# Combinations in four steps, gating two iterations behind its products, and work moved between engines in a two-layer hybrid trunk

## The chip, the cores and the metric

The kernel runs on 1 core of one Trainium2 chip. The metric is the device time of one execution in microseconds (us); smaller is better. Engines are named as in the profile: PE is TensorE, DVE is VectorE, ACT is ScalarE, POOL is GpSimd, and SP is the engine that issues most DMAs.

## What is computed

Two trunk layers over 1024 latent and 128 context tokens of width 1024, in fp32. What matters here, from the reference:

```python
def modulate(x, shift, scale):
    return layer_norm(x) * (1 + scale) + shift
# each of the two layers:
#   h = LN(x) * (1 + scale1) + shift1
#   cols = h @ w_in -> four mixers of 256 channels: mLSTM, pooling, gated MLP, SSD
#   x = LN_1(alpha * x + gate1 * (concat(mixer outputs) @ w_out))
#   h = LN(x) * (1 + scale2) + shift2
#   up-projection to 2 * 2816 -> centred depthwise conv (3) -> SiLU gate -> down-projection
#   x = LN_2(alpha * x + gate2 * ConvFFN(h))
```

## The kernel before, in words

**Tiling.** There are nine token tiles of 128 (tiles 0 to 7 latent, tile 8 context). Activations that feed products lie transposed in two SBUF buffers, `HH` (the part of a value that the fast fp32 product keeps) and `HL` (the rest); weights are split the same way by `wprep` (L141 to L143: DMA into `wr`, cast to `wh` on ACT, difference `wl` on POOL or DVE), and each product is three matmuls: high by high, high by low, low by high. Moving operands are 512 columns wide in most stages and HB = 290 in the FFN's up-projection; HT = 580 is two of those.

**Order.** A scheduler sets the order of each engine's instructions from the order of the code and a model of the times; `pin` keeps the instructions it is put around in the order of the code. Each engine then runs its own list in that order, so that an instruction that waits holds up all behind it. DMAs stand in the lists too: nearly all on SP, nine of the first layer on ACT.

**A layer, stage by stage**, with the lines that are touched:

- *Gating* (the loop over i in 0 to NT that calls `gate_mm`, `gate_a`, `ssd_y`, `ssd_e`, `gate_b`). `gate_mm` is 24 matmuls of 512 columns. `gate_a` takes their tanh and makes the gates. `ssd_y` sums the SSD's output of tile i in `yp`. `gate_b` of the tile before multiplies by the gate (L904), sums squares (L907), scales (L912), transposes on PE (L917) and writes the tile's columns of `HH` and `HL` (L919 to L924). The pooled and gated parts are loaded from DRAM (`pg`) and only split.
- *Out-projection and LN1* (loop after `project`): `project` makes a tile's product with `wo`, `residual` adds the input (L986, L987) and takes statistics, `affine` normalises and applies gain (DVE, L992) and bias (POOL, L993), stores x, a second norm follows on ACT (L250), and `to_ht` transposes (L262), modulates (L272), fills `HH` and `HL` (L274, L277) and spills the tile to DRAM as `hs` (L276, a DMA on SP). `stats` ends on POOL: a power (L221) and the negated product of mean and rstd (L233).
- *Up-projection.* Two of the 22 feature tiles f (`NP = 2`) are computed plainly. The other 20 are computed by `seven`, with seven half products in place of eight; those need sums and differences of activation parts. `combos` makes these from `hs`: per (b, kp) two row tiles `hr` are loaded with four DMAs (L1036, L1037) of 290 KB, four DVE operations combine them (L1046 to L1049), and `hi_lo` splits three results into TH and TL (L1027, L1028; one low part on DVE, two on POOL). Four further calls ("first") load x1 and x3 again and write their difference over the second half of HH and HL (L1042). `pieces` prepares the weight sums of an f on POOL (`sw`, L1092) and DVE. `conv` is the depthwise convolution.
- *Down-projection*: 7 groups of feature tiles by 9 token tiles. Between tiles a generator `ada` computes modulation vectors by steps (loads `wa` of 256 KB, then matmuls L199 and L207). It has 60 steps in layer 0 (20 for this layer, 40 for the next) and 20 in layer 1. Three steps are taken per two tiles from the third group on; what is left is drained at once before the second-last group.
- *LN2* in the last group: residual (zr, L1336; the add L1337 on DVE for the first half of the columns and on POOL for the second), statistics, gain and bias, then in layer 0 the next layer's norm and `to_ht`, in layer 1 the output. `stats` uses DVE's bn_stats (L227); `stats_s` has ACT sum the values and the squares (L240, L242). Layer 0 uses `stats` throughout, layer 1 `stats_s` for tiles 0 to 6.

## Time and profile before

| | |
|---|---|
| median of 3 runs | 2888.89 us (2887.58 to 2893.52) |
| profiled execution, its own time | 2894.44 us |
| its span in the trace | 2892.7 us |
| mean granted TensorE clock | 0.971 of full speed |
| PE busy | 2735.3 us, 95% |
| DVE busy | 1872.7 us, 65% |
| POOL busy | 1184.3 us, 41% |
| ACT busy | 1082.3 us, 37% |

The profile is of one execution. The clock of TensorE has two levels here, 2.4 GHz (shown as 1.00) and 1.2 GHz (0.50). PE counts as busy while a matmul is in flight, at either level, so that a PE that is 95% busy can still lose more than 5%: the number of matmuls in a stretch tells more than the busy time. A wait in the trace is put down to the instruction that released it.

### The profile page before, as it was taken

To read this page: it belongs to the slowest core of one execution; us is meant where nothing else is said; L and a number is where in the kernel's file an instruction comes from. 1 tells how busy PE (TensorE), PEld (TensorE's weight loads), DVE (VectorE), ACT (ScalarE), POOL (GpSimd) and SP (SyncE) were. 2 spreads that over 40 slices of the span, in tenths; PEclk is the share of its full clock that TensorE was granted. 3 is DMA by queue.
4 is the path that set the end of the run, shared out by engine and by line. 5 is a ranking of instruction groups with operands and counts; after the bars stand their busy time and mean duration, and the time that the engine had idled before them with its cause. 6 is when DMAs were issued, how large, how long until landed. Compare 5 with 4: busy or idle time off the path is not lost. (4 is left out here: it accounts for less than half of the span.)

```text
span 2892.7 us, 42560 instructions
## 1 busy us (share of the span) xinstructions
PE 2735.3 (95%) x16432; PEld 2415.6 (84%) x16432; DVE 1872.7 (65%) x3093; ACT 1082.3 (37%) x1960; POOL 1184.3 (41%) x903
## 2 busy tenths in 40 slices
PE   7999998998999999999979999989989999999996
PEld 2888886788999999877668889767889999998785
DVE  4736759565877777443495476685478777764347
ACT  3522343264444444411054234333553444443113
POOL 2534635364333332221484365354543333323137
PEclk9999999999999999999999999999999999999998
DMA  6334332444222223443523343324542222235323
GB/s 247 112 117 137 111 97 77 152 147 130 90 77 69 69 69 113 182 136 120 165 89 90 118 127 104 108 81 153 148 128 77 81 72 69 69 138 181 121 67 117
DMA packets 164891, 329.28 MB, mean 114 GB/s; under 512 B 23408, under 2 KB 81296, under 8 KB 164688
## 3 DMA queue, kind: packets, MB, share of 16 engines
q1 hardware_dynamic: 163392, 321.84, 34.1%
q10 hardware_dynamic: 1296, 4.72, 0.4%
q8 instruction: 129, 2.11, 0.3%
q14 instruction: 74, 0.61, 0.1%
HBM read 257.00 MB, written 69.50 MB: 113 GB/s over the span
## 5 line engine op out<-in xcount | busy, mean ns | idle before, releaser
L147 PE MATMUL ps<-wl,HH 128*128 128x512 f32 (+1 forms) x1152 | 394.3, 391 | 2.3 <-POOL wl L143 2.3
L147 PE MATMUL ps<-wh,HL 128*128 128x512 f32 (+1 forms) x1152 | 388.8, 392 | 5.5 <-POOL HL L277 5.5
L147 PE MATMUL ps<-wh,HH 128*128 128x512 f32 x1080 | 373.5, 401 | 13.1 <-ACT wh L142 8.8
L143 POOL TENSOR_TENSOR wl<-wr,wh 128x1024 fp32r<-128x1024 f32 (+2 forms) x80 | 204.8, 2564 | 347.6 <-ACT wh L142 320.5
L155 PE MATMUL pf<-HH,wh 128*128 128x386 f32 (+2 forms) x928 | 313.6, 338 | 2.7 <-DVE bt L654 2.7
L147 PE MATMUL pf<-HL,wh 128*128 128x386 f32 (+2 forms) x928 | 308.4, 332 | 0.0
L147 PE MATMUL pf<-HH,wl 128*128 128x386 f32 (+2 forms) x928 | 307.7, 332 | 0.0
L1115 PE MATMUL ps<-th,wh 128*128 128x290 f32 x960 | 287.0, 299 | 8.0 <-ACT th L1027 5.5
L1115 PE MATMUL ps<-tl,wh 128*128 128x290 f32 x960 | 287.8, 300 | 1.6 <-DVE tl L1028 1.6
L1115 PE MATMUL ps<-th,wl 128*128 128x290 f32 x960 | 287.3, 299 | 0.0
L147 PEld LDWEIGHTS ps<-wh,HH 128*128 128x128 f32 x1080 | 203.5, 190 | 76.1 <-DVE acc L1262 11.8
L147 PEld LDWEIGHTS ps<-wh,HL 128*128 128x128 f32 x1152 | 218.7, 190 | 54.9 <-POOL HL L277 7.0
L147 PEld LDWEIGHTS ps<-wl,HH 128*128 128x128 f32 x1152 | 219.4, 191 | 50.7 <-POOL wl L143 2.7
L1262 DVE TENSOR_TENSOR acc<-acc,ps 128x512 f32<-128x512 f32 x180 | 115.6, 682 | 198.3 <-PE ps L147 198.3
L1092 POOL TENSOR_TENSOR sw<-wr 128x512 f32<-128x512 f32 x40 | 56.4, 1409 | 440.2 <-DMA wr<-in_wup 258.3
L1115 PE MATMUL ps<-HH,wh 128*128 128x290 f32 x640 | 192.0, 300 | 4.2 <-DVE s L1143 4.2
L1115 PE MATMUL pf<-HH,wh 128*128 128x290 f32 x640 | 190.8, 299 | 3.6 <-ACT HH L1027 3.6
L1115 PE MATMUL pf<-HL,wh 128*128 128x290 f32 x640 | 191.4, 299 | 2.5 <-POOL HL L1028 2.5
L1115 PE MATMUL ps<-HL,wh 128*128 128x290 f32 x640 | 191.6, 299 | 0.0
L1115 PE MATMUL ps<-HH,wl 128*128 128x290 f32 x640 | 191.3, 299 | 0.0
L1115 PEld LDWEIGHTS ps<-th,wh 128*128 128x128 f32 x960 | 183.0, 191 | 9.5 <-ACT th L1027 6.0
L1115 PE MATMUL pf<-HH,wl 128*128 128x290 f32 x640 | 190.0, 297 | 0.0
(338 smaller groups left out, 6856.8 us busy)
## 6 DMA issues: line engine op xcount, KB each, us to landing
wr<-in_wup SPq DMA_DIRECT2D x88, 512.0 KB
wa<-in_w_ada SPq DMA_DIRECT2D x160, 256.0 KB
act<-cv SPq DMA_DIRECT2D x44, 577.0 KB
ar<-act SPq DMA_DIRECT2D x44, 577.0 KB
wr<-in_wdn SPq DMA_DIRECT2D x44, 512.0 KB
e<-rb SPq DMA_DIRECT2D x72, 256.0 KB
wr<-in_wfm SPq DMA_DIRECT2D x28, 512.0 KB
hr<-hs SPq DMA_DIRECT2D x48, 290.0 KB
```

The source lines that it names most:

```text
L143: eng.tensor_tensor(lo[:, :n], raw, hi.bitcast(F32)[:, :n], SUB)
L147: T.matmul(out, l, r, start=start, stop=stop)
L155: b = T.matmul(out, whk, xh, start=k == 0, stop=False)
L1092: G.tensor_tensor(s1, rv[:, h0], rv[:, h1], ADD)
L1115: T.matmul(out, x[:, ks], y[:, k], start=first and k + n == 0, stop=k == 3 and n == 2, skip_group_check=not first)
L1262: V.tensor_tensor(o, o, p[h], ADD)
```

## The change

Eight edits, all in one step:

1. `stats` and `stats_s` end on DVE instead of POOL (the negated mean times rstd, and the mean).
2. The spill of `to_ht` is issued from ACT's list instead of SP's; in the last iterations of LN1 the transposes are pinned.
3. `gate_b` runs two iterations behind `gate_a`; its loads move with it, into buffers of their own (`load_pg`).
4. `project` takes a list of tiles, and tiles 0 and 1 go side by side over k.
5. The bias of LN1 is added on DVE for tiles 7 and 8.
6. The plain product of f = 0 moves into LN1's last two iterations.
7. `combos` keeps every part in a small buffer of its own: 16 loads per layer instead of 24, all issued in one go; the difference x1 that the combinations need is also what goes over the second half of HH and HL, so that nothing is loaded again. Two of three low parts are made on DVE. The sum tile `sw` is one buffer, and the last combination borrows it.
8. `ada` takes two steps after each tile from the second group on; LN2 adds both halves and all biases on DVE and uses `stats_s` for tiles 0 to 6 in both layers.

```diff
@@ stats, stats_s
-        G.tensor_scalar(nm, mv[:, 0:1], rs, -1.0, MUL, MUL)
+        V.tensor_scalar(nm, mv[:, 0:1], rs, -1.0, MUL, MUL)
...
-        G.tensor_scalar(sums[:, 0:1], sums[:, 0:1], -1.0 / D, None, MUL)
+        V.tensor_scalar(sums[:, 0:1], sums[:, 0:1], -1.0 / D, None, MUL)
...
-        G.tensor_tensor(nm, sums[:, 0:1], rs, MUL)
-        return rs, nm
+        V.tensor_tensor(nm, sums[:, 0:1], rs, MUL)
+        return rs, nm, sums[:, 0:1]
@@ to_ht
-                T.transpose(p[:, j * P:(j + 1) * P], xh[:, (4 * h + j) * P:(4 * h + j + 1) * P], ident)
+                hold(T.transpose(p[:, j * P:(j + 1) * P], xh[:, (4 * h + j) * P:(4 * h + j + 1) * P], ident))
...
-                Q.dma_start(out=spill[:, ks, c0:c0 + P], in_=hf)
+                S.dma_start(out=spill[:, ks, c0:c0 + P], in_=hf)
@@ gating
-            pg = [mp.tile([P, 2, P], F32, tag="kt", name="pg", bufs=3) for _ in range(2)]
...
-            Q.dma_start(out=pg[0], in_=pl_d[l][:, :, tok(i)])
-            Q.dma_start(out=pg[1], in_=gu_d[l][:, :, tok(i)])
...
+        def load_pg(i):
+            pg = [mp.tile([P, 2, P], F32, tag=t, name="pg", bufs=n) for t, n in (("kt", 3), ("hs", 2))]
+            Q.dma_start(out=pg[0], in_=pl_d[l][:, :, tok(i)])
+            Q.dma_start(out=pg[1], in_=gu_d[l][:, :, tok(i)])
+            return pg
...
-            if i > 0:
-                gate_b(i - 1, *ga.pop(i - 1))
+            if 1 <= i <= NT:
+                pgs[i - 1] = load_pg(i - 1)
+            if i > 1:
+                gate_b(i - 2, ga.pop(i - 2), pgs.pop(i - 2))
@@ out-projection, LN1
+        def project(tiles):
+            ps_ = [[ps(), ps()] for _ in tiles]
             for k in range(KD):
...
+                for i, p in zip(tiles, ps_):
...
-            G.tensor_tensor(x, x, lnb, ADD)
+            (V if i >= 7 else G).tensor_tensor(x, x, lnb, ADD)
...
+            if i == 0:
+                pq[0], pq[1] = project((0, 1))
+            elif 1 < i < NT:
+                pq[i], = project((i,))
...
+            if i == NT:
+                plain(0, 0)
...
+            if i > NT:
+                plain(0, 1)
+                plain(0, 2)
...
+                to_ht(l, 1, i - 2, z, op, pf if i < NT else ps, spill=hs_d[l],
+                      **({"hold": pin} if i >= NT else {}))
@@ combinations
+        def combos(b, r):
             t1, t2 = slice(HB * b, HB * (b + 1)), slice(HT + HB * b, HT + HB * (b + 1))
...
+            for kp in range(2):
+                n = 2 * b + kp
+                ka, kb = slice(2 * kp, 2 * kp + 2), slice(4 + 2 * kp, 6 + 2 * kp)
...
+                for dst, ks, t in ((x1, ka, t1), (x3, ka, t2), (x2, kb, t2), (x4, kb, t1)):
+                    Q.dma_start(out=dst, in_=hs_d[l][:, ks, t])
+                pin(V.tensor_tensor(x1, x3, x1, SUB))
+                V.tensor_tensor(x3, x2, x3, SUB)
+                V.tensor_tensor(x2, x2, x1, SUB)
+                V.tensor_tensor(x4, x2, x4, SUB)
+                for j, x, eng in ((0, x2, V), (1, x3, G), (2, x4, V)):
+                    hi, lo = tbuf(6 * n + 2 * j), tbuf(6 * n + 2 * j + 1)
+                    hi_lo(hi, lo, x, eng)
...
-            s1, s4 = (up_.tile([P, 512], F32, tag="sw", name="sw", bufs=2) for _ in range(2))
+            s1, s4 = halves(sum_tile())
...
+        plain(1, 0)
         nxt = []
         prep = pieces(NP, nxt)
         next(prep)
+        plain(1, 1)
+        plain(1, 2)
+        t1s = [row_tile("hr").rearrange("p (k c) -> p k c", k=4) for b in range(2)]
+        for b in range(2):
+            combos(b, t1s[b])
+        plain(0, 3)
+        plain(1, 3)
         next(prep)
         for b in range(2):
-            for kp in range(2):
-                combos(b, kp, False)
+            t2 = slice(HT + HB * b, HT + HB * (b + 1))
+            hi_lo(HH[:, 0:4, t2], HL[:, 0:4, t2], t1s[b])
...
-        for b in range(2):
-            for kp in range(2):
-                combos(b, kp, True)
@@ down-projection, LN2
-                    if gi > 1:
+                    if gi > 0:
                         next(ada, None)
-                        if i % 2:
-                            next(ada, None)
+                        next(ada, None)
...
-                        (G if h else V).tensor_tensor(o[:, hs], o[:, hs], z, ADD)
-                    rq[i - 1] = stats(o, tp) if more or i >= CTX else stats_s(o, tp)
+                        V.tensor_tensor(o[:, hs], o[:, hs], z, ADD)
+                    rq[i - 1] = stats_s(o, tp) if i < CTX else stats(o, tp)
...
-                        (G if i % 2 else V).tensor_tensor(o, o, lnb, ADD)
+                        V.tensor_tensor(o, o, lnb, ADD)
```

Lines of the changed kernel have larger numbers than those of the kernel before (L276 stays, L912 becomes L915, L993 becomes L1000, L1115 becomes L1146). Three places of the order follow.

SP's list in layer 0, from the end of LN1 on, before (`hs` written by L276 is the spill, `hr` the loads for the combinations, `wr` weights, `xmid` the stored x):

```order
L276 DMA hs_85<-hf 128x4x128
L141 DMA wr<-in_wup 128x1024
L1077 DMA wr<-in_wup 128x1024
L1078 DMA wr<-in_wup 128x1024
L276 DMA hs_85<-hf 128x4x128 x2
L994 DMA xmid_71<-x 128x1024 x2
L276 DMA hs_85<-hf 128x4x128 x4
L1036 DMA hr<-hs_85 128x2x290
L1037 DMA hr<-hs_85 128x2x290
```

The same place of SP's list now (`tc`, `hr` and `sw` are all loads of parts for the combinations):

```order
L141 DMA wr<-in_wup 128x1024 x2
L1074 DMA sw<-hs_85 128x2x290
L1108 DMA wr<-in_wup 128x1024
L1001 DMA xmid_71<-x 128x1024
L1109 DMA wr<-in_wup 128x1024
L1001 DMA xmid_71<-x 128x1024
L1074 DMA tc<-hs_85 128x2x290
L1074 DMA hr<-hs_85 128x2x290
L1074 DMA tc<-hs_85 128x2x290 x2
```

The spills have left the list, and the loads stand right behind the two last stores of x.

PE's list in layer 0 where `ada` was drained before the second-last group of the down-projection, before:

```order
L147 MATMUL ps<-wh,HL 128x512 x2
L207 MATMUL ps<-pairs,wa 128x2 x4
L199 MATMUL ps<-wa,condw 32x512 x8
L207 MATMUL ps<-pairs,wa 128x2 x4
L199 MATMUL ps<-wa,condw 32x512 x8
L207 MATMUL ps<-pairs,wa 128x2 x4
L147 MATMUL ps<-wh,HH 128x512 x2
```

PE's list now, around the last steps of `ada` in layer 0:

```order
L199 MATMUL ps<-wa,condw 32x512 x2
L147 MATMUL ps<-wh,HH 128x512
L147 MATMUL ps<-wl,HH 128x512
L147 MATMUL ps<-wh,HL 128x512
L147 MATMUL ps<-wh,HH 128x512 x2
L147 MATMUL ps<-wl,HH 128x512
```

No two groups of L199 stand together any more; the products of a token tile lie between them.

PE's list in layer 0 where the first f of `seven` meets its first combination, before:

```order
L1115 MATMUL ps<-HL,wh 128x290
L1115 MATMUL ps<-HH,wl 128x290
L1115 MATMUL ps<-th_5975,wh 128x290
L1115 MATMUL ps<-tl_5978,wh 128x290
L1115 MATMUL ps<-th_5975,wl 128x290
```

The same meeting now:

```order
L1146 MATMUL pf<-HL,wh 128x290
L1146 MATMUL pf<-HH,wl 128x290
L1146 MATMUL ps<-tc,wh 128x290 x6
L1146 MATMUL ps<-tc,wl 128x290
L1146 MATMUL ps<-tc,wh 128x290
```

Before, the half product just ahead of the combination's was the first one on plain activations; now three of the plain ones (the last of them on the difference in HH and HL, in `pf`) come ahead of it.

## Rows read from the trace of the kernel before

**Rows 1.** Stretches: us, busy of PE, PEld, DVE, ACT, POOL (instructions), clock, DMA, GB/s.

```profile
430.00:522.00 92.00, 78.45 (x398) 64.77 (x397) 82.66 (x157) 34.52 (x88) 47.91 (x45) 0.93 0.27 83
626.00:640.00 14.00, 8.86 (x46) 8.26 (x45) 10.99 (x12) 8.73 (x15) 12.19 (x10) 0.76 0.62 174
690.00:740.00 50.00, 40.19 (x236) 38.37 (x235) 41.29 (x48) 25.58 (x38) 19.67 (x12) 0.83 0.44 135
800.00:850.00 50.00, 50.00 (x375) 50.00 (x375) 39.56 (x47) 20.70 (x32) 18.38 (x10) 1.00 0.20 67
1374.00:1395.00 21.00, 16.00 (x51) 5.32 (x52) 2.32 (x6) 2.10 (x3) 4.97 (x4) 0.67 0.71 234
1460.00:1512.00 52.00, 37.70 (x207) 32.05 (x206) 49.30 (x87) 32.56 (x68) 47.30 (x45) 0.87 0.27 102
...
2052.00:2066.00 14.00, 9.03 (x45) 8.21 (x44) 10.50 (x11) 8.32 (x14) 12.16 (x11) 0.76 0.61 182
2120.00:2160.00 40.00, 29.80 (x180) 27.86 (x179) 32.72 (x33) 20.07 (x30) 18.03 (x11) 0.87 0.41 130
2839.00:2868.00 29.00, 28.77 (x124) 22.88 (x122) 25.66 (x34) 18.00 (x27) 24.63 (x25) 1.00 0.18 70
2868.00:2893.00 25.00, 0.00 (x0) 0.00 (x0) 20.24 (x24) 6.45 (x9) 19.14 (x14) 0.54 0.31 126
```

**Rows 2.** What PE waited for over the span: us in total, times, longest us.

```profile
PE ps L917 <- DVE yp L912: 19.8, 18, 3.0
...
PE pf L262 <- ACT z L250: 10.1, 2, 5.1
...
PE pf L262 <- ACT acc L250: 5.8, 4, 2.1
```

**Rows 3.** One line, DVE's L907 in gating: shortest, median and longest ns.

```profile
L907 DVE SCALAR_TENSOR_TENSOR th<-yp x36: 275/292/2364, 440.8 to 1941.1; 128x128 f32<-128x128 f32 x36
```

**Rows 4.** PE's timeline at LN1's end, layer 0: start us, us, idle before.

```profile
632.49 1.97 PE L262 MATMUL pf<-ident,z 128*128 128x128 f32 x8 [5.14 <-ACT z L250]
```

**Rows 5.** ACT's timeline there.

```profile
629.12 1.06 ACT L142 ACTIVATE wh<-wr 128x1024 fp32r<-128x1024 f32 x1 [0.96 <-DMA wr<-in_wup]
...
631.21 1.23 ACT L250 ACTIVATE z<-x,nm,rs 128x1024 f32<-128x1024 f32 x1
```

**Rows 6.** SP's timeline behind LN1, layer 0: the first load for the combinations.

```profile
661.36 0.46 SPq L1036 DMA_DIRECT2D hr<-hs  x1
```

**Rows 7.** What DVE waited for from 640 to 740: us, times, longest.

```profile
DVE hr L1046 <- DMA hr<-hs: 22.2, 3, 18.5
```

**Rows 8.** What PE waited for from 690 to 740, its longest wait.

```profile
PE ps L1115 <- ACT th L1027: 2.8, 1, 2.8
```

**Rows 9.** PE's timeline at `ada`: between tiles (1325.89), then drained.

```profile
1325.89 1.07 PE L199 MATMUL ps<-wa,condw 128*32 128x512 f32 x8
...
1373.15 0.95 PE L207 MATMUL ps<-pairs,wa 128*128 128x2 f32 x8
1374.03 1.38 PE L199 MATMUL ps<-wa,condw 128*32 128x512 f32 x8
1378.99 4.56 PE L199 MATMUL ps<-wa,condw 128*32 128x512 f32 x8 [3.58 <-DMA wa<-in_w_ada]
...
1386.03 6.94 PE L199 MATMUL ps<-wa,condw 128*32 128x512 f32 x16
...
1394.62 0.70 PE L147 MATMUL ps<-wh,HH 128*128 128x512 f32 x2
```

**Rows 10.** One line, LN2's add on either engine: shortest, median, longest ns.

```profile
L1337 DVE TENSOR_TENSOR acc<-acc,zr x18: 632/681/2041, 1442.6 to 2874.4; 128x512 f32<-128x512 f32 x18
L1337 POOL TENSOR_TENSOR acc<-acc,zr x18: 1264/1676/2337, 1442.8 to 2875.7; 128x512 f32<-128x512 f32 x18
```

**Rows 11.** DVE's timeline, its last operation.

```profile
2887.43 1.28 DVE L1345 SCALAR_TENSOR_TENSOR acc<-acc,rs,lnb 128x1024 f32<-128x1024 f32 x1 [0.44 <-POOL rs L221]
```

**Rows 12.** ACT's timeline in layer 1's LN2, one square with its sum.

```profile
2858.18 1.15 ACT L242 ACTIVATE junk<-acc,sums 128x1024 f32<-128x1024 f32 x1 [3.50 <-POOL sums L241]
```

More of the change, by code (lines that the diff above doesn't have):

```diff
@@ L245, in stats_s, with to_ht @@
         nm = pl.tile([P, 1], F32, tag="nm", name="nm", bufs=2)
-        G.tensor_tensor(nm, sums[:, 0:1], rs, MUL)
-        return rs, nm
+        V.tensor_tensor(nm, sums[:, 0:1], rs, MUL)
+        return rs, nm, sums[:, 0:1]
     def norm(out, z, rn):
         S.activation(out, z, AF.Identity, bias=rn[1], scale=rn[0])
-    def to_ht(l, which, i, xh, pl, psf=None, both=False, dve=False, spill=None):
+    def to_ht(l, which, i, xh, pl, psf=None, both=False, dve=False, spill=None, hold=lambda b: b):
         c = 0 if i < CTX else 1
@@ L939, in layer @@
         YP = big(4, [P, 4, 2, 256], "yp")
-        ga = {}
-        for i in range(NT + 1):
+        ga, pgs = {}, {}
+        for i in range(NT + 2):
             if i + 1 < NT:
@@ L992, in affine, with row_tile, plain @@
             V.tensor_tensor(x, x, lng, MUL)
-            G.tensor_tensor(x, x, lnb, ADD)
+            (V if i >= 7 else G).tensor_tensor(x, x, lnb, ADD)
             Q.dma_start(out=xmid[l][i * P:(i + 1) * P, :], in_=x)
+        NP = 2
+        w0, u0 = {}, {}
+        def row_tile(name="row"):
+            return up_.tile([P, NCOL], F32, tag="row", name=name, bufs=6)
+        def plain(f, j):
+            if f not in w0:
+                w0[f] = [wprep(a["wup"][l, f + NF * part], eng=G if f else V) for part in range(2)]
+                u0[f] = row_tile("ug"), row_tile("uv")
+            for part in range(2):
+                p = pf()
+                fm(p[:, 0:HB], w0[f][part], HB * j, HB)
+                S.activation(u0[f][part][:, HB * j:HB * (j + 1)], p[:, 0:HB], AF.Copy)
         pq, st1 = {}, {}
         for i in range(NT + 2):
-            if i < NT:
-                pq[i] = project(i)
+            if i == 0:
+                pq[0], pq[1] = project((0, 1))
+            elif 1 < i < NT:
+                pq[i], = project((i,))
             if i == CTX:
@@ L1019, in layer @@
         tpl = ts.enter_context(pool("tcomb"))
-        TH = [tpl.tile([P, 4, HT], F32R, name=f"th{j}") for j in (2, 3, 4)]
-        TL = [tpl.tile([P, 4, HT], F32R, name=f"tl{j}") for j in (2, 3, 4)]
-        def row_tile(name="row"):
-            return up_.tile([P, NCOL], F32, tag="row", name=name, bufs=6)
         def hi_lo(hi, lo, src, eng=V):
@@ L1028, in hi_lo, with tbuf @@
             eng.tensor_tensor(lo, src, hi.bitcast(F32), SUB)
[L1030 to L1051 removed]
+        def tbuf(n, dt=F32R):
+            return (up_ if n < 4 else tpl).tile([P, 2, HB], dt, tag=f"t{n}", name="tc", bufs=1)
@@ L1114, in product @@
                 for n, (x, y) in enumerate(((wh, xh), (wh, xl), (wl, xh))):
-                    T.matmul(out, x[:, ks], y[:, k], start=first and k + n == 0, stop=k == 3 and n == 2,
+                    T.matmul(out, x[:, ks], y[k], start=first and k + n == 0, stop=k == 3 and n == 2,
                              skip_group_check=not first)
@@ L1150, in seven @@
                 yield
-        NP = 2
-        w0 = [[wprep(a["wup"][l, f + NF * part], eng=G if f else V) for part in range(2)] for f in range(NP)]
-        u0 = [(row_tile("ug"), row_tile("uv")) for f in range(NP)]
+        plain(1, 0)
         nxt = []
@@ L1343, in layer @@
                         rs, _, mean = rq[i - 1]
-                        V.scalar_tensor_tensor(o, o, mean, lng, SUB, MUL)
+                        V.scalar_tensor_tensor(o, o, mean, lng, ADD if i < CTX else SUB, MUL)
                         V.scalar_tensor_tensor(o, o, rs, lnb, MUL, ADD)
```

57 lines of the change are left out of this document (17 added, 40 removed).

## The prediction

> **What bounds the kernel now.** I began with the stretches [rows 1], because the busy shares of the whole span hide where PE loses. In the steady up-projection, 800 to 850, PE issues 375 matmuls of 290 columns in 50 us, 0.133 us each, at full clock: nothing of the change touches that, and most of the kernel is like it. The reader should look for stretches with fewer matmuls than time and a clock under 1.00. They are: gating (430 to 522 and its twin in layer 1), the end of LN1 (626 to 640, 2052 to 2066), the start of `seven` (690 to 740, 2120 to 2160), the drained `ada` (1374 to 1395), LN2 of layer 0 (1460 to 1512) and the tail after the last matmul (2868 to 2893). Then I read what PE waits for [rows 2]: L912 of the gating in 18 pieces of about 1.1 us, the norm before the transposes of LN1 in two pieces of 5.1 us, and the norm of LN2. Each stage of the change answers one of these waits, so the sum goes stage by stage, and its base is the profiled execution (2894.44 us), 5.5 us over the median of the runs.
>
> **`ada`, two steps a tile.** Drained, it fills PE's list from 1374.03 to 1394.62, 20.6 us, with 32 matmuls L199 and 16 L207; it waits 3.58 us for a weight load and runs much of it at half clock [rows 9], the clock of the stretch being 0.67 [rows 1]. Between tiles, eight L199 cost 1.07 us and eight L207 0.95 us [rows 9]. So the same 48 cost 4.3 + 1.9 = 6.2 us: **14.5 us** gained, once (layer 1 has 20 steps and drains nothing in either kernel). It holds only if the `wa` loads land within the tile that lies between steps; 72 slots for 60 steps leave none to drain. Range 12 to 15.
>
> **Combinations.** In 690 to 740 PE issues 236 matmuls; at 0.133 us those are 31.4 us, so 18.6 of 50 are lost; by the same count 16.1 of 40 in layer 1 [rows 1]. The longest single wait is for the high part of a combination [rows 8], and behind it stands DVE, which waited 22.2 us for `hr` loads [rows 7]; the first was issued at 661.36, behind the four last spills [rows 6]. Now the spills are in ACT's list, the loads are 16 instead of 24 and stand behind the last stores of x; I put their start some 12 us earlier. The four operations on DVE and the split follow as before; four subtractions and four low parts on POOL (the "first" calls) are gone. And the three plain half products come first on PE, which covers about 72 matmuls of the wait. Against it: DVE's list is in order, and the combinations stand before the convolution and the weight differences; `sw` is one buffer, and the last combination holds it, so that the sums of the first f wait for that. Following this chain by hand, the last weight of the first f is ready some 6 us after PE wants it, and a stall of that length costs about 3 us more at half clock (after the 5.1 us wait in LN1 [rows 4], the stretch's clock is 0.76). So 9 to 10 of 18.6 are left, and I take **9 us** a layer, 18 in all. Bounds: 2 a layer (the weights no sooner than now), 16 (nothing lost).
>
> **End of LN1.** PE waits 5.14 us for the norm of tile 6 [rows 4] and then runs slow (mean clock 0.76 [rows 1]), some 2 us more: about 7 lost. Layer 1 shows the same stretch (2052 to 2066). The norm at 631.21 stands behind two weight casts on ACT, the second of which ends at 630.2 having waited for its load [rows 5]; that load was queued on SP behind a spill. Now no spill stands on SP, DVE makes the last scalar in place of POOL, and POOL's power comes ahead of a low part. How much sooner the load lands can't be read here; it lies between nothing and the whole wait, and I take half, 2.5 us, and 1.5 less at half clock: **4 us** a layer, 8 in all. The plain product of f = 0 that moves here is still behind the transposes in PE's list, so it fills nothing in this wait. Bounds 0 and 7. The spills cost ACT 18 issues a layer of at most 0.46 us, as the loads take on SP [rows 6]; ACT is busy 8.73 of 14 us there [rows 1], so they are covered, and if that cover went, the price would be two of them before the last norm, 0.9 us.
>
> **Gating.** DVE is busy 82.66 of 92 us, PE 78.45 with the clock at 0.93 [rows 1]. With a lag of two, the transposes on PE need a scaling that DVE did an iteration before, so the 19.8 us of waits [rows 2] go. What is late next is DVE itself: its operations and their order are the same, and the end of the stage needs the last of them, since the rows for LN1 are loaded only after the last transpose. So PE can only win back what DVE stands idle, 92 - 82.66 = 9.3 us, of which some is needed to start and to end: **4 us** a layer, 8 in all; bounds -3 (one more iteration at the end) and 9. L907 takes 292 ns in the median and up to 2364 [rows 3]: DVE is stretched by something that runs beside it. The Trainium skill ("SBUF — State Buffer", section "Who interferes with whom") says that a DVE operation with two inputs in SBUF contends with a POOL operation that reads SBUF, and that one of them then blocks for its whole length. L907 is such an operation, and the spread in [rows 3] agrees; by that rule alone the lag would give 0 here, not 8, and the sum would end 8 us higher. It is part of rival (b).
>
> **LN2 of layer 0.** DVE is busy 49.30 of 52 us while PE issues 207 matmuls [rows 1]: DVE sets the pace, about 7.4 us a tile. Per tile (0 to 6) it gives up two bn_stats halves (some 0.6 each, like the add) and an aggregate, takes one more half add (0.63 [rows 10]) and three small ones: -0.4. POOL gives up a 1.68 us add that ran beside DVE's, and DVE's own add (0.68 median, 2.04 at the longest [rows 10]) and gains are less stretched: -0.6. Over nine tiles that is 8 to 9; but ACT takes a copy and a square of 1.15 us each [rows 12], 16 us for seven tiles on top of 32.56 busy in 52 [rows 1], and its list is in order. I take **6 us**; bounds -5 and 10.
>
> **Tail.** The last matmul ends at 2868; DVE works from 2839 to 2888.7 [rows 11], 45.9 us of it busy [rows 1]. Now it has 36 half-width operations (0.63), 18 of full width (1.28), four bn_stats (0.63 too) and 27 small ones of some 0.1: 22.7 + 23.0 + 2.5 + 2.7 = 50.9 us, undisturbed by POOL, against 49.7 that the stretch takes: **1 us lost**; bounds 4 lost and 2 gained.
>
> **Nothing.** Tiles 0 and 1 side by side: their matmuls were interleaved by the scheduler already, and the waits there are for weight loads whose place on SP is the same. The bias of tiles 7 and 8 on DVE is part of the combination's chain. Other stages keep their order but for single swaps.
>
> **The sum.** 14.5 + 18 + 8 + 8 + 6 - 1 = 53.5 us. 2894.4 - 53.5 = 2840.9 for a profiled run, 5.5 less for the median: **2835 us**.
>
> **The rivals.**
> (a) The combinations' gain turns into a new wait: the first f's sums wait for `sw` until the last combination is done. PE's new plain half products speak against it, DVE's strict list for it. 2 instead of 9 a layer: 2849.
> (b) Gating and LN2 stay where they are: DVE blocked by POOL in the one, ACT the bound in the other. Gating by itself: L907's median is 0.292 us and its longest 2.364 [rows 3], and where DVE's time is made by POOL's operations beside it, a lag that moves none of them gives 0 instead of 8, 2843; that is also what the page named above would make of it. With ACT's 16 us at LN2 giving -3 instead of 6 it is 2852; with (a) too, 2866.
> (c) All that PE loses at the start of `seven` and DVE's whole idle time in gating come back: 7 more and 5 more a layer, 2811.
> (d) Slower: the whole of DVE's list waits on the loads. In the kernel before, the 22 us wait stood where PE still had plain products to do. If the last loads (they need the last spills, now behind the norms and modulations on ACT) land late, the combinations hold up the convolution and the weight differences of the first f, and not even the first half product can start. With 22 us plus its half clock, 30 a layer in place of the gain of 9, the time is 2835 + 2 x 39 = 2913. It decides from about 27 us a layer, that is, if the last combination ends past 720 instead of the 696 that I put it at.
> (e) Nothing changes that can be measured: the edits' gains are given back at the next wait. 2889. Against it: the drained `ada` has nothing behind it that would take its 14.5 us back.
>
> **Chances.** Forecast 0.50, within 2815 to 2848 by itself; (a) 0.17, (b) 0.13, both 0.04; (c) 0.07; (d) 0.05; (e) 0.04. A measurement of this kernel can tell about 0.2%, 6 us, from no change. Faster by more: the forecast, (a), (b), both and (c), 0.91, less 0.02 for losses I haven't seen, half of which goes to each side: 0.89. Within 0.2%: (e), 0.05 with that. Slower: (d), 0.06 with that. The range from 2803 to 2868 leaves out (d), (e) and the ends of (c) and of (a) with (b).
>
> **What the changed profile would show.** `ada`: no two groups of L199 back to back, no stretch at half clock before the second-last group. Combinations: the first load at about 649, PE's stall before the first f's product with `tc` under 8 us, and some 300 matmuls in 50 us there. LN1: a wait of about 2.5 us for z. Gating: no waits for the scaling, and DVE over 90% busy. LN2: about 6.7 us a tile. Wrong would be: a long idle stretch of DVE before the combinations with PE idle at the same time (d), or PE's waits for ACT's norm in LN2 longer than 5.8 us in all [rows 2].

## The result, and the profile of the changed kernel

The changed kernel takes **2861.64 us** (median; 2853.45 to 2863.46), beside 2891.20 us (the median of four runs) for the kernel before: a ratio of 0.989, interval [0.9862, 0.9917]. It is 30 us faster, where the prediction had 54 (2889 to 2835): the direction and the range were right, and the gain was about half of the forecast. Profiled execution against profiled execution it is 34 us (2860.52 beside 2894.44), and the account below goes by these.

The stretches of the changed kernel that answer to [rows 1], with the same columns (us, busy of PE, PEld, DVE, ACT, POOL with instructions, clock, DMA share, GB/s). They are gating, LN1's end, the start of `seven`, the place of the drained `ada`, LN2 of layer 0 with the wait at its end, the start of `seven` in layer 1, and the tail:

```profile
430.00:522.00 92.00, 79.35 (x413) 65.83 (x411) 80.99 (x157) 34.51 (x90) 49.68 (x46) 0.93 0.27 84
620.00:634.00 14.00, 10.57 (x54) 9.71 (x53) 12.48 (x14) 11.50 (x23) 11.92 (x8) 0.76 0.75 220
690.00:740.00 50.00, 41.44 (x284) 40.85 (x285) 41.38 (x48) 18.72 (x29) 21.59 (x12) 0.90 0.23 84
1374.00:1395.00 21.00, 21.00 (x92) 17.02 (x92) 15.05 (x14) 0.91 (x1) 13.14 (x8) 1.00 0.36 112
1436.00:1488.00 52.00, 40.09 (x216) 34.56 (x215) 48.34 (x95) 41.94 (x85) 34.13 (x28) 0.84 0.24 91
...
2090.00:2130.00 40.00, 29.85 (x201) 28.79 (x200) 32.24 (x35) 16.72 (x27) 17.97 (x10) 0.87 0.22 83
2836.00:2859.00 23.00, 0.30 (x2) 0.00 (x0) 18.76 (x31) 6.14 (x9) 5.12 (x4) 0.59 0.34 137
```

The `ada` stretch is full (92 matmuls in 21 us instead of 51, clock 1.00), the start of `seven` has 284 matmuls where it had 236, and LN2 has 216 in 52 us where it had 207. What PE waits for over the span, beside [rows 2]:

```profile
PE pf L1146 <- ACT wh L1053: 10.8, 2, 5.4
PE ps L505 <- DVE r L477: 10.7, 2, 5.4
PE ps L920 <- DVE yp L893: 8.6, 2, 4.3
PE ps L147 <- ACT wh L142: 8.4, 2, 4.9
PE ps L147 <- POOL HL L277: 7.5, 8, 2.8
PE pf L262 <- ACT z L250: 7.0, 2, 3.5
...
PE pf L1146 <- DVE wl L1054: 6.3, 2, 3.1
...
PE ps L920 <- DVE yp L915: 2.7, 1, 2.7
```

Of the 18 waits for a scaling (L912, now L915) one is left, and the wait for LN1's norm is down from 10.1 to 7.0. Two waits are new. At the top is L1146: the first f of `seven` waits for its weight sums, 5.4 and then 3.1 us in each layer. The other is L920, 4.3 us in each layer: the last transposes of the gating wait for a product that DVE makes (`yp`, L893).

To place the 34 us, I use the **lead**: both kernels issue 16432 matmuls, and the lead at a point of the trace of before is the start of the n-th matmul in that trace less the start of the n-th in the other one. Stages that the change leaves alone keep it within some tenths, so its steps tell where time was gained. Inside a stage whose order was changed, the n-th matmul is another product in each trace; there, only the step over the whole stage counts. The last matmul is at 2867.4 before and at 2836.0 after, a lead of 31.4.

| term of the sum | forecast | lead from, to (layer 0; layer 1) | measured |
|---|---|---|---|
| gating, with the out-projection's start | 8 | -1.1, 4.0; 23.3, 26.5 | 8.3 |
| end of LN1 | 8 | 4.0, 5.9; 26.5, 28.6 | 4.0 |
| combinations, start of `seven` | 18 | 5.9, 10.5; 28.6, 31.5 | 7.5 |
| `ada` | 14.5 | 10.1, 23.3 | 13.2 |
| LN2 of layer 0 | 6 | 23.3, 23.1 | -0.2 |
| tail (span less last matmul) | -1 | 25.3 us before, 22.7 after | 2.6 |
| sum | 53.5 | | 35.4 |

The rest to 34.0 is the first 420 us (-1.1) and tenths. Those 420 us are nearly the same work in every kernel here, and the lead at their end lay between -2.1 and 2.5 in 12 of 13 profiles (-4.9 in e10), so a lead is known to some 2 us from one profile to the next; a step within one stage is read more closely.

### The profile page after: what moved, and what is told of

Same layout as the page of the kernel before. It is cut to its first block, busy times and chain, and to the rows that moved or that the text cites. A ratio compares the mean times of both kernels' runs of the same rounds, so it can differ in the third digit from the quotient of the medians.

```text
span 2858.7 us, 42460 instructions
## 1 busy us (share of the span) xinstructions
PE 2715.9 (95%) x16432; PEld 2405.3 (84%) x16432; DVE 1897.1 (66%) x3188; ACT 1094.5 (38%) x1984; POOL 1091.4 (38%) x782
## 4 chain that ended last, share of the span: by engine, by line
PE 78%; DVE 11%; issue 3%; DMA 3%; POOL 3%; ACT 2%; SPq 0%; POOLq 0%; DVEq 0%; ACTq 0%
PE ps L1146 22%; PE ps L147 22%; PE pf L147 11%; PE pf L1146 9%; PE pf L155 5%; PE ps L199 2%; PE pf L168 1%; PE ps L610 1%; PE ps L352 1%; DMA wr<-in_wout 1%; DMA e<-rb 1%; DVE th L910 1%; DVE yp L907 1%; PE ps L803 1%; POOL acc L1331 1%
## 5 line engine op out<-in xcount | busy, mean ns | idle before, releaser
L1146 PE MATMUL ps<-tc,wh 128*128 128x290 f32 x1920 | 389.4, 297 | 0.0
L143 POOL TENSOR_TENSOR wl<-wr,wh 128x1024 fp32r<-128x1024 f32 (+2 forms) x80 | 204.4, 2558 | 345.6 <-ACT wh L142 332.6
L1146 PEld LDWEIGHTS ps<-tc,wh 128*128 128x128 f32 x1920 | 310.7, 189 | 0.0
L1146 PE MATMUL ps<-tc,wl 128*128 128x290 f32 x960 | 284.7, 297 | 0.0
L147 PEld LDWEIGHTS ps<-wh,HH 128*128 128x128 f32 x1080 | 203.8, 190 | 76.0 <-DVE acc L1288 10.9
L1146 PE MATMUL pf<-HH,wh 128*128 128x290 f32 x640 | 192.7, 301 | 10.8 <-ACT wh L1053 10.8
L1146 PE MATMUL pf<-HH,wl 128*128 128x290 f32 x640 | 191.2, 299 | 6.3 <-DVE wl L1054 6.3
L1053 ACT ACTIVATE wh<-wr 128x512 fp32r<-128x512 f32 x200 | 121.6, 626 | 189.5 <-PE ps L1146 162.9
L1146 PE MATMUL ps<-HH,wh 128*128 128x290 f32 x640 | 190.3, 297 | 3.2 <-ACT s L1167 3.2
L1146 PE MATMUL pf<-HL,wh 128*128 128x290 f32 x640 | 192.5, 301 | 0.0
L1146 PE MATMUL ps<-HH,wl 128*128 128x290 f32 x640 | 190.1, 297 | 0.0
L1146 PE MATMUL ps<-HL,wh 128*128 128x290 f32 x640 | 189.7, 296 | 0.0
```

The source lines that it names most:

```text
L143: eng.tensor_tensor(lo[:, :n], raw, hi.bitcast(F32)[:, :n], SUB)
L147: T.matmul(out, l, r, start=start, stop=stop)
L1053: S.activation(hi, src, AF.Copy)
L1146: T.matmul(out, x[:, ks], y[k], start=first and k + n == 0, stop=k == 3 and n == 2, skip_group_check=not first)
```

## The experiments

Every ratio is to the kernel before in the same group of runs. e1 to e4 ran together (before 2892.90), e5 to e8 (2895.86), and e9 to e12 (2892.79).

**e1: `ada` alone, in the kernel before.**

```diff
-                    if gi > 1:
+                    if gi > 0:
                         next(ada, None)
-                        if i % 2:
-                            next(ada, None)
+                        next(ada, None)
```

> The kernel before with one part of the change: ada takes two steps after each tile from the second group on. Theory: the drained steps have nothing behind them that takes their time back; the time falls by 13 to 15 us (ratio about 0.995), PE shows no half clock near 1374, and the start of LN2 comes 13 us sooner. Rival: the steps cost as much between tiles (loads that don't land within a tile); under 5 us.

Measured: 2882.46 us, 0.9963 [0.995, 0.9976]. The lead rises to 12.6 at 1400 and stands there until LN2; by 1600 it is 9.3 and at the end 7.9. So the step gives what it should at its place, and in this kernel, though not in the changed one, some 5 us go again behind it. The groups of waits of e1 and of before between 1440 and 1900 differ by no one item of that size; where the 5 us went stays open.

**e2: the gating's lag of two alone, in the kernel before.**

```diff
-            if i > 0:
-                gate_b(i - 1, *ga.pop(i - 1))
+            if 1 <= i <= NT:
+                pgs[i - 1] = load_pg(i - 1)
+            if i > 1:
+                gate_b(i - 2, ga.pop(i - 2), pgs.pop(i - 2))
... (and `load_pg`, as in the change)
```

> The kernel before with one part of the change: gate_b two iterations behind gate_a, its loads moved with it. Theory: PE gets about 9 us ahead within the loop, since it no longer waits for the scaling, and loses about 6 of them again at the start of the out-projection, whose last weights are loaded only after the last transposes: 3 to 5 us a layer stay, 6 to 10 in all. Rival: what the loop gains stays, 9 a layer, 18 in all.

Measured: 2885.49 us, 0.9975 [0.9964, 0.9986]. In layer 0 the lead goes from -2.1 at 420 to 10.5 at 507 and is back at 1.8 by 519: most of what PE gets ahead in the loop is gone when the loop ends. The changed kernel does the same (-1.1, 12.0, then 3.0 from 516 to 534). Its PE timeline at the end of the gating and the start of the out-projection (start us, us, idle before):

```profile
507.14 0.66 PE L920 MATMUL ps<-ident,yp 128*128 128x128 f32 x2 [4.28 <-DVE yp L893]
...
522.93 0.50 PE L147 MATMUL ps<-wh,HH 128*128 128x512 f32 x1 [1.41 <-DVE HL L923]
...
536.55 2.50 PE L147 MATMUL ps<-wh,HH 128*128 128x512 f32 x5 [3.56 <-ACT wh L142]
```

PE ends its last gating product at 497.3 and then waits for DVE three times, 1.87, 1.44 and 4.28 us, before the last SSD output and the transposes that follow it. DVE is busy almost without a gap there (the columns of the stretches above):

```profile
494.00:508.60 14.60, 7.01 (x34) 5.28 (x33) 14.39 (x32) 5.84 (x13) 7.53 (x7) 0.78 0.12 37
```

So it is DVE that sets the end of the gating. The expectation had the size right (7.4 us by the medians), but its reason, the late out-projection weights, is not what the trace shows: the lead has fallen to 3.0 before that wait begins at 533.0. The kernel before has the same wait:

```profile
PE ps L147 <- ACT wh L142: 8.8, 2, 4.9
```

In the changed kernel it is 8.4 us. What that weight waits for is seen in the changed kernel's timelines of SP and of ACT (the cast to `wh`):

```profile
505.74 8.72 SPq L141 DMA_DIRECT2D wr<-in_wout  x4
521.54 0.80 SPq L965 DMA_DIRECT2D g<-gate  x2
522.40 0.42 SPq L965 DMA_DIRECT2D lng<-in_lnp  x1
522.87 0.43 SPq L965 DMA_DIRECT2D lnb<-in_lnp  x1
523.34 1.79 SPq L991 DMA_DIRECT2D x<-xin  x3
525.22 1.75 SPq L141 DMA_DIRECT2D wr<-in_wout  x2
```

```profile
522.04 2.00 ACT L142 ACTIVATE wh<-wr 128x1024 fp32r<-128x1024 f32 x2
...
535.44 1.06 ACT L142 ACTIVATE wh<-wr 128x1024 fp32r<-128x1024 f32 x1 [11.39 <-DMA wr<-in_wout]
```

The last two weight tiles come through two shared raw buffers (`wr`), so their loads are issued at 525.22, when the two before them have been cast (522.04 to 524), behind seven loads of 512 KB, and land at 535.4.

**e5: those two tiles in raw buffers of their own, and all six loads ahead of the rows** (in the changed kernel):

```diff
-        raw = wp.tile([P, D], F32, tag="wr", name="wr", bufs=2)[:, :n]
+        raw = (rp or wp).tile([P, D], F32, tag="wr", name="wr", bufs=2)[:, :n]
@@ the six wout loads, written ahead of g1l, g1c, lng, lnb
+        wo += [wprep(..., rp=opw if k >= 6 else None) for k in range(WB, KD)]
```

> The changed kernel, but the last two weight tiles of the out-projection get load buffers of their own and all six are loaded ahead of the rows for LN1. Theory: what the loop of the gating wins (PE is 9 us ahead at 500) is given back at the start of the out-projection because those two loads wait for the casts of the two before them, which stand on ACT behind the split of the last transposes; with own buffers the 3.6 us wait for the cast shrinks and 3 to 6 us a layer are kept. Rival: the loads wait for the memory that the gating frees with its last transposes, so that they come no sooner; within 2 us a layer of the changed kernel.

Measured: 2845.04 us, 0.9833 [0.9815, 0.9851]. SP now issues all six loads in one go,

```profile
505.57 10.09 SPq L141 DMA_DIRECT2D wr<-in_wout  x6
```

PE's wait for `wh` there is gone, and the lead goes from -0.7 to 10.9 over gating and the out-projection's start, and from 31.3 to 42.0 in layer 1: 11.6 and 10.7 instead of 5.1 and 3.2. But at the end of the gating the lead has fallen to 3.6 here too (layer 0, 516 to 531), as in the changed kernel; it rises to 10.3 by 546, at the place of the wait for `wh`. So e5 does not keep what the gating had won. It takes away a wait that the kernel before had as well, together with the slow clock behind it: from 520 to 545 e5 has 103 matmuls at a clock of 1.00, the changed kernel 81 at 0.93.

**e3: the last combination's fourth part not in `sw`** but in the later `s2` buffer (in the changed kernel):

```diff
-  ([view(sum_tile(), [P, 2, HB])] if n == 3 else [])
+  ([up_.tile([P, 2, HB], F32, tag="s2", name="s2")] if n == 3 else [])
... (and the two `s2` tiles of an f become one of that shape)
```

> The changed kernel, but the last combination's fourth part lies in the buffer that the first f's second sum uses later, instead of in the buffer of the weight sums, so that POOL can make the weight sums of the first f at once. Theory: the stall of PE before the third half product (5.4 us for the cast of a weight sum, 3.1 for its low part, then half clock) comes from that buffer being held; it goes, and 7 to 10 us a layer are gained against the changed kernel: about 2846. Rival: the chain is set by ACT's list, in which the casts of the combinations stand behind the copies of the plain products; then PE waits for the combinations instead, and under 3 us a layer are gained.

Measured: 2841.49 us, 0.9824 [0.98, 0.9848]. What it mends, in the changed kernel's timelines of DVE, POOL, ACT and PE:

```profile
693.23 0.75 DVE L1054 TENSOR_TENSOR tc<-sw,tc 128x580 fp32r<-128x580 f32 x1
```

```profile
694.06 2.32 POOL L1123 TENSOR_TENSOR sw<-wr 128x512 f32<-128x512 f32 x1 [4.71 <-DVE tc L1054]
```

```profile
696.54 0.61 ACT L1053 ACTIVATE wh<-sw 128x512 fp32r<-128x512 f32 x1
```

```profile
697.21 0.61 PE L1146 MATMUL pf<-HH,wh 128*128 128x290 f32 x1 [5.42 <-ACT wh L1053]
...
701.68 0.61 PE L1146 MATMUL pf<-HH,wl 128*128 128x290 f32 x1 [3.14 <-DVE wl L1054]
```

It reads as one chain: the last low part reads `sw` until 694.0, POOL's first weight sum of the first f may then write `sw`, ACT casts it, and PE, which has stood since 691.8, goes on at 697.2. With the part elsewhere, POOL makes its sums earlier, and PE waits for little between 640 and 740 (e3, total, times, longest):

```profile
PE ps L1146 <- DVE s L1172: 1.6, 1, 1.6
PE pf L1146 <- ACT wh L1053: 1.0, 1, 1.0
PE ps L1146 <- DVE tc L1054: 0.9, 1, 0.9
PE pf L1146 <- DVE uv L1178: 0.4, 1, 0.4
```

The stretch from 690 to 740 of e3 holds 335 matmuls at full clock, where the changed kernel has 284 at 0.90:

```profile
690.00:740.00 50.00, 46.04 (x335) 44.93 (x334) 46.09 (x55) 19.97 (x31) 17.62 (x9) 1.00 0.23 79
```

The lead goes from 7.0 to 20.4 there and from 40.8 to 51.5 in layer 1, 24.1 in all instead of 7.5. Layer 0's part of that can be followed. PE's waits between 640 and 740 fall from 10.1 us (5.4, 3.1 and 1.6) to 3.9, which is 6.2. Behind the stall the changed kernel runs slow, as the two stretches of 11 us after it show:

```profile
702.00:713.00 11.00, 11.00 (x67) 11.00 (x67) 7.17 (x8) 1.26 (x2) 3.08 (x3) 0.78 0.41 149
713.00:724.00 11.00, 11.00 (x84) 11.00 (x84) 7.60 (x15) 5.33 (x9) 3.17 (x3) 1.00 0.28 95
```

17 matmuls fewer at 0.131 us are 2.2 us. The two make 8.4 of the 8.8 by which the step of the lead grew (13.4 less 4.6).

**e6: the spill back on SP** (`S.dma_start` to `Q.dma_start` in `to_ht`, in the changed kernel).

> The changed kernel with the spill of LN1 issued from SP's list again. Theory: the spills hold up SP's list, so the up-projection's first weights and the loads of the combinations come later: the wait for the norm of tile 6 is back at 5 us (2 a layer lost), and the combinations' first subtraction, at 644.8 in the changed kernel, comes 8 to 15 us later; as ACT's list and the weight sums set their end, PE loses under 4 us a layer more. Rival: the loads decide; PE loses 9 or more a layer.

Measured: 2860.16 us, 0.9883 [0.9863, 0.9903], no different from the changed kernel. The move does bring the loads forward: without it, DVE's first combination waits for its loads (e6, 640 to 740),

```profile
DVE hr L1075 <- DMA hr<-hs: 16.4, 1, 16.4
```

and with it 2.3. But in the changed kernel DVE then stands at the next place of its list,

```profile
662.34 2.20 DVE L1054 TENSOR_TENSOR tc<-tc 128x580 fp32r<-128x580 f32 x2 [12.76 <-ACT tc L1053]
```

for ACT, whose cast (661.04) stands behind copies of the plain products, and these PE gives out one in 3.2 us. The loads were early, and the wait had only moved: the last low part is at 694.1 in e6 and at 693.2 in the changed kernel. The wait for LN1's norm is 3.4 us in e6 as in the changed kernel, so the spill is not what shortened it either.

**e10: the statistics' last scalar back on POOL** (`V` to `G` in the three lines of the first edit).

> The changed kernel with the last scalar of the statistics back on POOL (three lines), nothing else. The spill's move had been worth nothing at the end of LN1, where PE's wait for z fell from 5.1 to 3.4 us. Theory: the scalar on DVE is what shortened that wait. Then z's wait is back at 4.5 to 5.1 us, and PE loses some 2 us a layer there, 1 to 3 more in layer 1's tail, so 2866 to 2869 us. Rival: the order around it (DVE's bias for the last tiles, the plain product) shortened it; then the wait stays at 3.4 and the time within 3 us of the changed kernel.

Measured: 2856.86 us, 0.9878 [0.9863, 0.9892]: no different. PE's waits for z are 7.3 us in two pieces, beside 7.0, but the pieces differ: 2.8 us in layer 0 and 4.5 in layer 1, beside 3.4 and 3.5. Layer 1 alone is as the theory has it, layer 0 goes the other way. So the spill's move did not shorten LN1's wait (e6), and for the scalar on DVE it is not shown. What is plain is only what stood in front of the norm before and what does now. Before, ACT stood 2.74 and 0.96 us for the loads of the two weights just ahead of it (the second is in [rows 5]); now ACT's timeline has no wait for a load:

```profile
622.32 1.09 ACT L142 ACTIVATE wh<-wr 128x1024 fp32r<-128x1024 f32 x1
623.27 1.28 ACT L250 ACTIVATE x<-z,nm,rs 128x1024 f32<-128x1024 f32 x1
624.40 0.67 ACT L274 ACTIVATE HH<-hf 128x512 fp32r<-128x512 f32 x1
624.92 1.27 ACT L250 ACTIVATE z<-x,nm,rs 128x1024 f32<-128x1024 f32 x1
```

The norm (624.92) has its scalar from DVE at 622.7 and stands behind three other operations of ACT. Which edit brought the weight loads forward wasn't tried, and the late load may not be the whole cause: in layer 0 of e10 ACT waits 1.86 us for a load again, and PE's wait is the shorter one.

**e11: the first two out-projection tiles one after the other again** (in the changed kernel).

```diff
-            if i == 0:
-                pq[0], pq[1] = project((0, 1))
-            elif 1 < i < NT:
+            if i < NT:
                 pq[i], = project((i,))
```

> The changed kernel with the first two tiles of the out-projection written one after the other as before, nothing else. Theory of the prediction: worth nothing, the scheduler interleaves the two tiles either way and the waits there are for weights; the time stays within 3 us of 2861 and the waits for the last two out-projection weights are the same within 1 us. Rival: side by side hides a part of those weights' arrival; then PE falls 3 to 7 us a layer further behind at the out-projection's start, 2868 to 2875.

Measured: 2857.91 us, 0.9879 [0.9864, 0.9894]; PE's waits for `wh` of L142 are 8.7 us in all beside 8.4. As predicted, the step is worth nothing: by the names of what they read and write, PE's matmuls stand in the same order as in the changed kernel in all but 12 of 16432 places, so the scheduler interleaves the two tiles whichever way they are written.

**e4: layer 0's LN2 with bn_stats on DVE again** (in the changed kernel).

```diff
-                    rq[i - 1] = stats_s(o, tp) if i < CTX else stats(o, tp)
+                    rq[i - 1] = stats(o, tp) if more or i >= CTX else stats_s(o, tp)
...
-                        V.scalar_tensor_tensor(o, o, mean, lng, ADD if i < CTX else SUB, MUL)
+                        V.scalar_tensor_tensor(o, o, mean, lng, SUB, MUL)
```

> The changed kernel, but LN2 of layer 0 takes its statistics with bn_stats on DVE in all tiles, as before the change (the adds stay on DVE). Theory: ACT bounds that stage now (it is busy over 8 of 10 us from 1446 on), so without its two sums per tile the stage gets shorter by 3 to 8 us. Rival: DVE bounds it as before, and the stage gets longer by 4 to 8 us.

Measured: 2859.11 us, 0.9881 [0.9861, 0.99], no different; the lead over LN2 goes from 26.4 to 24.4. DVE is then busy without a gap:

```profile
1413.90:1484.80 70.90, 57.51 (x275) 48.37 (x273) 70.83 (x141) 32.28 (x65) 33.95 (x28) 0.88 0.23 89
```

Giving ACT the statistics (41.9 of 52 us busy in the changed kernel, not a bound by itself) gives DVE some air there, and it is worth 2 us, no more.

**e12: LN2 of layer 0 without POOL's low parts.** The 18 subtractions that make the low part of layer 1's input are left out, so layer 1 reads stale ones.

```diff
-            G.tensor_tensor(HL[:, ks, c0:c0 + P], hf, ..., SUB)
+            if which or not l:
+                G.tensor_tensor(HL[:, ks, c0:c0 + P], hf, ..., SUB)
```

> The changed kernel without the low parts that POOL makes for layer 1's input in layer 0's LN2 (18 subtractions of 128x512, so that layer 1 uses stale low parts there). In that stretch DVE's operations take 6.2 us more than their medians (18 adds by 0.15, 9 second gains by 0.25, 9 first gains by 0.14 on the average). Theory: POOL's operations beside them stretch them; then the second gains fall to 1.28 us, the first to 1.27, the adds to 0.68, and LN2 from the first zr to the last affine operation on DVE takes 62 to 63 us in place of 68.4, the kernel 2855 or 2856. Rival: the stretch comes from elsewhere (ACT reading the same rows, loads); then it stays at 67 or more, and the kernel within 2 us of the changed one.

Measured: 2854.29 us, 0.9865 [0.9849, 0.9882], about 3 us under e10 and e11 of the same group. The gains lost their stretch as the theory said, and the adds' mean in this stage fell from 823 to 738 ns; one pair of adds is still 2.35 us long instead of 1.28, at 1449.99, beside a weight difference that POOL makes from 1449.20 to 1451.20 (L143). One line each, LN2's second gain in the changed kernel and in e12 (L1371 there), shortest, median and longest ns:

```profile
L1370 DVE SCALAR_TENSOR_TENSOR acc<-acc,rs,lnb x11: 1266/1278/2167, 1426.1 to 2853.9; 128x1024 f32<-128x1024 f32 x11
```

```profile
L1371 DVE SCALAR_TENSOR_TENSOR acc<-acc,rs,lnb x11: 1271/1275/1279, 1424.3 to 2847.5; 128x1024 f32<-128x1024 f32 x11
```

In the changed kernel the product that reads PSUM (L1361) keeps its time beside POOL, and the add, which reads SBUF twice, does not:

```profile
L1361 DVE TENSOR_TENSOR zr<-ps,g x36: 628/680/692, 1417.0 to 2840.4; 128x512 f32<-128x512 f32 x36
```

```profile
L1362 DVE TENSOR_TENSOR acc<-acc,zr x36: 665/680/1897, 1418.2 to 2842.9; 128x512 f32<-128x512 f32 x36
```

But the stage is as long as before: from the first zr to the start of the last gain it takes 68.3 us, as against 68.4. DVE now waits for ACT's squares (e12, 1415 to 1485), which it did for 0.9 us in the changed kernel:

```profile
DVE rs L220 <- ACT junk L242: 4.0, 2, 2.0
```

PE fared better than DVE, its lead going from 25.4 to 28.3 at 1540 and 29.6 at 1600. So both readings of LN2 hold a part: POOL's low parts stretch DVE, and where they are gone ACT's list is next, so that of the 6.2 us of stretch 3 to 4 come back.

**e7: layer 1's LN2 with the second half's add and the odd biases on POOL again** (in the changed kernel).

```diff
-                        V.tensor_tensor(o[:, hs], o[:, hs], z, ADD)
+                        (G if h and not more else V).tensor_tensor(o[:, hs], o[:, hs], z, ADD)
...
-                        V.tensor_tensor(o, o, lnb, ADD)
+                        (G if i % 2 else V).tensor_tensor(o, o, lnb, ADD)
```

> The changed kernel, but in layer 1's LN2 the second half's add and every other bias go to POOL as before the change. Theory: the 22.7 us from the last matmul to the end grow by 2 to 4, to the 25.3 of the kernel before, since POOL's adds of 1.3 to 2.3 us and its powers stand in the chain of the last tiles. Rival (the prediction's sum): DVE has less to do, and the tail is 1 us shorter.

Measured: 2867.02 us, 0.991 [0.9888, 0.9932]; the tail from the last matmul (2836.8) to the end of the span (2864.7) is 27.9 us, 5.2 longer than the changed kernel's. DVE's timeline shows both reasons, two operations at 1.6 and 3.3 us that take 0.68 and 1.27 elsewhere, and the last power on POOL, which the last gain needs, behind a bias:

```profile
2844.74 1.63 DVE L1362 TENSOR_TENSOR acc<-acc,zr 128x512 f32<-128x512 f32 x1
...
2846.36 3.29 DVE L1369 SCALAR_TENSOR_TENSOR acc<-acc,mv,lng 128x1024 f32<-128x1024 f32 x1
...
2859.75 0.21 DVE L233 TENSOR_SCALAR nm<-mv,rs 128x1 f32<-128x1 f32 x1 [2.74 <-POOL rs L221]
```

**e8: the mends of e3 and e5 together**, and ACT's statistics in layer 0's LN2 for tiles 0 to 3 only.

> The changed kernel with three edits: the last combination's fourth part in its own buffer, the out-projection's last weights with own load buffers, and ACT's statistics in layer 0's LN2 for tiles 0 to 3 alone, bn_stats from tile 4 on. Theory: the first gives 20 us as measured, the second 6 to 12, the third 2 to 4, since ACT has nothing to do while the first tiles pass and is full later: 2841 less 8 to 16, 2825 to 2833. Rival: LN2 is bound by the sum of what ACT and DVE have to do, so that a share between them changes nothing, and the second does nothing: 2841.

Measured: **2829.44 us**, 0.9779 [0.9762, 0.9797], the fastest of all, 32 us under the changed kernel. The leads add up stage by stage: 10.8 and 10.2 in gating with the out-projection's start, 13.5 and 11.1 at the combinations, 13.1 at `ada`; the third edit brings nothing (39.5 to 37.7 over LN2).

**e9** was to be e8 with tiles 0 to 6 on ACT. The kernel that ran lacks the raw buffers of its own that its expectation speaks of: of e5's edit it has only the loads written ahead of the rows, beside e3's.

> The changed kernel with the two mends that were timed one by one: the last combination's fourth part in a buffer that is needed later (not in sw), and own raw buffers for the last two out-projection loads. All tiles 0 to 6 of layer 0's LN2 keep ACT's statistics. Theory (the two stalls are independent, each is paid once a layer): the gains add, 20.2 + 16.6 = 36.8 us below the changed kernel, so 2825 us; matmul for matmul some +11 a layer at the out-projection's start and +12 to +13 a layer at the first combination. Rival (the same two with bn_stats for tiles 4 to 6 ran at 2829, and a gain in one place is partly given back at the next): 2830 or more.

Measured: 2843.82 us, 0.983 [0.9816, 0.9845], the time of e3. It so tells something else than it was made for: without buffers of their own the last two loads stay where they were in SP's list, however early they are written,

```profile
526.18 1.74 SPq L141 DMA_DIRECT2D wr<-in_wout  x2
```

and PE waits 4.0 us for them. In e5 it is the buffers that count. Whether e8 with tiles 0 to 6 on ACT would be faster still wasn't tried.

## Why the prediction was right in direction and half too large

By the time alone the result would be rival (a) together with (b), 2866. By the stages it is not: (b)'s 8 us for the gating were not lost, while 4 were at LN1's end, which neither of the two names; that the total came near 2866 is chance. Four terms were too high, by 10.5 (combinations), 6.2 (LN2), 4.0 (LN1) and 1.3 us (`ada`), and the tail was too low by 3.6.

- **`ada`: right.** 13.2 of 14.5, inside 12 to 15; 12.6 alone, in e1. No two groups of L199 stand together, and the stretch runs at full clock.
- **Combinations: the term was mis-sized, 7.5 instead of 18.** Rival (a) was the mechanism, and it had its place right: `sw`, held by the last combination. The forecast had put that in as a stall of 6 us and 3 at half clock, leaving 9 a layer; the stall was 8.6 us in two pieces (`wh`, then `wl`), and with the rest of its cost 4.6 and 2.9 were left. e3 shows the counterpart: with `sw` free the step is worth 13.4 and 10.7, more than the 9 that the sum had. The failed step is "following this chain by hand": it had the last weight of the first f 6 us late, without the second wait for `wl`, and had DVE's operations follow the loads "as before", where they stood 12.8 us behind one of ACT's casts. The start of `seven` got 284 matmuls in 50 us, not the 300 named.
- **The spill's move: worth nothing** (e6). DVE's first subtraction is at 644.83 with it and at 660.7 without (the first load at 640.25, before the 649 of the forecast), and DVE's next wait, for ACT, takes it all.
- **End of LN1: half, 4.0 instead of 8.** The wait went from 5.1 to 3.4, not to 2.5. The sum's reason, the late loads ahead of the norm, is what left ACT's timeline; that the spill's move did this did not stand in e6, and for DVE's scalar e10 says one thing in each layer. The cause stays open.
- **Gating: 8.3 of 8, and by the mechanism of the forecast.** "What is late next is DVE itself", and "the end of the stage needs the last of them": PE gets up to 12 us ahead in the loop of layer 0, then waits three times for DVE, which is busy 14.39 of 14.60 us, and 3.0 are left. Two of the signs were off: one wait for a scaling stayed (2.7 us), and DVE is busy 80.99 of the 92 us, 88% and not over 90%. The part on tiles 0 and 1 was right too in putting the wait for the weights at nothing, since it is the same in both kernels (8.8 and 8.4 us). That it could be taken away, for about twice what the lag gives, is what e5 adds (16.6 us).
- **Rival (b), the stretch beside POOL,** did not decide gating: the lag moved no POOL operation out of it and gained all the same, though the longest of the stretched line (L907, now L910) is still 2.29 us, beside 2.36 before. In LN2 the stretch is there, and e12 shows its cause: the second gain's longest falls from 2167 to 1279 ns when POOL's subtractions are left out, and in the changed kernel zr (L1361, one input in PSUM) is never over 692 ns where the add (L1362, both inputs in SBUF) reaches 1897. The Trainium skill ("SBUF — State Buffer", section "Who interferes with whom") says that a DVE operation with two SBUF inputs contends with a POOL operation that reads SBUF. By that rule the add and the gains should stretch and zr should not, and these traces agree.
- **LN2: -0.2 instead of 6.** The failed step is "gains are less stretched: -0.6" a tile: the mean of the second gain was 1470 ns before and is 1529 now, since the low parts still run beside it, and the adds on DVE cost 5.5 us more in all than before, with some 4 of small operations. What bn_stats gave up, 9.2, was spent on these. A tile takes 7.6 us (68.4 for nine), not 6.7. Rival (b)'s ACT bound is wrong: e4 loses 2, and PE's waits for ACT's norm in LN2 are 2.4 us, beside 5.8 before.
- **Tail: the sign was wrong, 2.6 gained instead of 1 lost.** The mis-sized term is DVE's work, 50.9 us in the sum and 46.86 in the trace, from the first product of layer 1's LN2 to the end of its last gain (columns as in [rows 1]):

```profile
2807.45:2855.20 47.75, 28.85 (x124) 22.92 (x122) 46.86 (x86) 24.46 (x35) 11.27 (x9) 0.84 0.24 95
```

The sum had added up durations, and an operation starts before the one ahead of it has ended: half-width ones of 0.68 us stand 0.60 us apart, and the gains and biases of tiles 0 to 6, of 1.21 us where the sum had 1.28, stand 1.14 apart. DVE is indeed the bound there, busy 46.86 of 47.75 us; before, it was 45.8 of 49.6 and had gaps. With POOL's share back, the tail is 5.2 us longer (e7).

- **Rival (d)** did not come: the last low part is at 693.2, where the forecast had put 696, well before the 720 from which it decides.

## What to carry to other kernels

Before a step that makes an engine arrive earlier is counted at its whole gain, look at what that engine needs next: three of the gains here (gating, the early loads, LN2) met the next late thing within one stage: DVE's own last products, an in-order cast, and another engine's list. And a wait that both kernels have does not show where one is compared with the other: that for the out-projection's weights, 8.8 us before and 8.4 after, was worth 16.6 us when e5 took it away. A buffer that is lent for a moment costs its next writer, not its borrower; so list who writes it next and how long the chain from there to the busiest engine is. When half of a forecast is missing, the lead by the n-th instruction of the busiest engine tells in which stage, and each stage then has a wait with a name.

## What the runs showed that was not expected

- Loads written early are not issued early if their buffers rotate: with two raw buffers the last two loads went out at 526 in e9 as at 525 in the changed kernel, and at 505.6 to 515.7 once they had their own (e5).
- A stall of PE at the start of `seven` cost a third more than its length: 6.2 us of waits and 2.2 at a clock of 0.78 behind them (layer 0, e3 beside the changed kernel).
- POOL's full-width operations stretch DVE's by up to 2.6 times where they meet (3.29 us for a gain of 1.27 in e7), yet 6 us of such stretch in LN2 were worth only 3 to 4 when removed.
